# Dilated attention heads laid out query by query, whole row-tiled pairs, and a table of shifts in the instruction order of a one-core transformer kernel

## The chip, the core and the metric

The kernel runs on one core of one Trainium2 chip. The metric is the device time of one execution in microseconds (us), and the time of a kernel is the median of several executions. In the profile the engines are called PE (TensorE, matrix products), PEld (its weight loads), DVE (VectorE), ACT (ScalarE), POOL (GpSimd) and SP (SyncE, which issues the DMA transfers).

## What is computed

A sequence of 512 tokens with 1024 channels goes through two blocks. The first has two layers: mixer AB and then mixer C, each followed by a convolutional FFN and a gated side input (PLE). The second has two hybrid layers. The change rewrites one half of mixer AB, the eight dilated heads of 64 channels; their mathematics is this:

```python
for window, dilation in A_PATTERNS:            # ((128, 1), (512, 4), (2048, 16))
    o, lse = dilated_window_attention(qf, kf, vf, window, dilation)
    outs.append(o)
    lses.append(lse)
w = jax.nn.softmax(jnp.stack(lses), axis=0)
o = jnp.sum(w[..., None] * jnp.stack(outs), axis=0)
```

Three windowed attentions weighted by their log sums are one attention in which a key that lies in n of the three windows counts n times. Both kernels compute it so: before by a factor n on the exponential, after by ln n added to the score. The other half of mixer AB are eight dense latent heads; mixer C is differential attention with 16 score maps.

## The kernel before

The data are feature-major: 128 channels by 512 tokens fill one tile. A large product is made of three products of high and low parts (`h`, `l` are the parts of a weight, staged by DMA into `st`, split by ACT into `h` and by DVE into `l`). The attention of dilated heads is key-major: `attn(j)` handles pair j of heads, j from 0 to 3. It stacks high and low parts of q and k (`stack`), gets each query's row maximum from a first pass of score products (`rowmax`, written to `mt`), transposes the maxima into a row of q (`rows`), and makes the scores a second time, transposed, 128 keys by 512 queries (`attend`). The exponential is then multiplied by the multiplicity `multa` on DVE (`post`), the products with V go to the bank `o`, and the sums of the exponentials come from an addition tree and one product with ones; `finish` divides. Mixer C is query-major: 128 queries by 512 keys, the score products of its two maps run in two 64-row tiles of PE side by side, then exponentials, transpositions through the identity (`identr`) and products with V.

Nothing is issued where it is written. `Rec.add` records every operation with its predecessors, `Rec.price` gives it a cost, and `Rec.order` is a list scheduler: of the operations that are ready on an engine it takes the one with the lowest key, which is the place in the program, or on PE in a small tile mode the lowest of the same mode. `Rec.issue` emits the result, so every row of the trace has line 619 and one goes by the names of the tiles: `d` are the three PSUM banks of dense products, `S` the two of scores, `o` the one of outputs, `m` the two of transpositions and the rest; `s` are slots in SBUF, `sm` small columns. `nc.pair()` links matmuls of two tiles that are to run side by side. The program's orders of steps (`ORDER_AB`, `ORDER_C`, `ORDER_H`) stand at the head of the file.

The stages in the trace of before are: mixer AB 0 to 326 us, FFN and PLE to 757, mixer C to 1036, FFN and PLE to 1470, the hybrid layers to 1961 and to the end.

## Time and profile before

| what | us |
|---|---|
| median of 3 executions | 2468.52 (2467.8 to 2470.66) |
| the profiled execution | 2466.22 |
| its span in the trace | 2464.1 |
| PE busy in the span | 2424.9 (98%) |
| DVE busy | 1462.3 (59%) |
| ACT busy | 1013.8 (41%) |
| POOL busy | 498.1 (20%) |
| mean granted clock of PE | 0.996 |

The profiled execution takes 2.1 us more than its span, and 2.3 us less than the median. A busy PE is one that has an instruction in it: matmuls overlap, a row of the timeline gives a start and a duration that runs into the next instruction, and the distance from one start to the next is what an instruction costs.

### The profile page before, as it was taken

What the parts mean: (1) busy time and instruction counts of PE and PEld (TensorE: products, weight loads), DVE (VectorE), ACT (ScalarE), POOL (GpSimd) and SP (SyncE); (2) the same over time, 40 slices, a digit from 0 to 9 for tenths busy, and PEclk for the clock granted to TensorE, in tenths of its full rate; (3) what the DMA queues carried; (4) which work ended last, traced back from release to release, by engine and by line L of the source; (5) the groups of instructions that cost most, each with busy time, mean ns of one, the idle gap of its engine ahead of it and who ended that gap; (6) DMA issues with size and microseconds to landing.
All of it is one profiled execution on the core that took longest, in us unless ns stands there. A gap on an engine that the chain in (4) does not pass through costs nothing.

```text
span 2464.1 us, 31052 instructions
## 1 busy us (share of the span) xinstructions
PE 2424.9 (98%) x12020; PEld 1934.7 (79%) x12020; DVE 1462.3 (59%) x2461; ACT 1013.8 (41%) x1692; POOL 498.1 (20%) x473
## 2 busy tenths in 40 slices
PE   8999999999999999999999999999999999999998
PEld 6655688888887777888888888776778887767787
DVE  5798675354474756664453676576553556665535
ACT  5554364243353545553342454433333344333332
POOL 1333221010131322211010230311122103111221
PEclk9999999999999999999999999999999999999999
DMA  5102123323323112232232243221232432213331
GB/s 176 52 26 72 59 86 99 98 95 98 100 76 124 52 56 74 85 101 96 94 101 96 86 145 100 78 74 47 93 113 95 167 97 75 77 43 94 113 95 66
DMA packets 73224, 220.26 MB, mean 89 GB/s; under 512 B 9525, under 2 KB 13621, under 8 KB 73078
## 3 DMA queue, kind: packets, MB, share of 16 engines
q1 hardware_dynamic: 73078, 218.30, 27.1%
q8 instruction: 94, 1.54, 0.2%
q14 instruction: 52, 0.43, 0.1%
HBM read 209.87 MB, written 8.39 MB: 89 GB/s over the span
## 4 chain that ended last, share of the span: by engine, by line
PE 89%; DVE 5%; ACT 3%; DMA 1%; issue 1%; POOL 1%; POOLq 0%; DVEq 0%; SPq 0%; ACTq 0%
PE d L619 72%; PE S L619 10%; PE o L619 4%; DVE s L619 4%; PE m L619 3%; ACT s L619 3%; DVE S L619 1%; POOL s L619 1%; DMA st<-in_abin 1%; DVE l L619 0%; DVE mt L619 0%; DVE sm L619 0%; DMA s<-in_p 0%; ACT h L619 0%; ACT sm L619 0%
## 5 line engine op out<-in xcount | busy, mean ns | idle before, releaser
L619 PE MATMUL d<-s,h 128*128 128x512 f32 (+2 forms) x5536 | 1674.6, 381 | 13.4 <-ACT h L619 6.1
L619 PEld LDWEIGHTS d<-s,h 128*128 128x128 f32 (+1 forms) x5536 | 1016.9, 188 | 235.1 <-issue 22.3
L619 PE MATMUL d<-s,l 128*128 128x512 f32 (+1 forms) x2768 | 1047.5, 378 | 0.9 <-DVE l L619 0.7
L619 DVE TENSOR_TENSOR l<-st,h 128x1024 fp32r<-128x1024 f32 (+4 forms) x379 | 473.6, 1252 | 548.0 <-ACT h L619 547.7
L619 ACT ACTIVATE h<-st 128x1024 fp32r<-128x1024 f32 (+4 forms) x379 | 389.2, 1027 | 865.8 <-PE d L619 693.4
L619 POOL TENSOR_TENSOR s<-s,s 128x512 f32<-128x512 f32 (+2 forms) x327 | 406.9, 1249 | 1086.2 <-DVE s L619 671.8
L619 PEld LDWEIGHTS d<-s,l 128*128 128x128 f32 x2768 | 521.4, 188 | 103.4 <-issue 8.0
L619 ACT ACTIVATE s<-s 128x512 f32<-128x512 f32 (+5 forms) x547 | 291.4, 548 | 382.9 <-DVE s L619 273.2
L619 DVE TENSOR_TENSOR s<-s,s 128x512 fp32r<-128x512 f32 (+6 forms) x373 | 215.2, 593 | 95.2 <-ACT s L619 76.4
L619 PE MATMUL S<-s,s 64*128 64x512 f32 (+8 forms) x752 | 197.6, 383 | 3.9 <-DVE mt L619 2.1
L619 PEld LDWEIGHTS S<-s,s 128*128 128x128 f32 (+4 forms) x752 | 112.0, 186 | 78.7 <-ACT s L619 33.7
L619 DVE TENSOR_TENSOR s<-d,s 128x512 f32<-128x512 f32 (+3 forms) x135 | 80.0, 593 | 115.4 <-PE d L619 113.0
L619 POOL TENSOR_SCALAR s<-s 128x512 f32<-128x512 f32 x44 | 29.2, 663 | 579.1 <-ACT s L619 579.1
L619 DVE SCALAR_TENSOR_TENSOR s<-s,s 128x512 f32<-128x512 f32 (+4 forms) x171 | 116.7, 697 | 40.8 <-ACT s L619 40.0
L619 PE MATMUL S<-s,h 128*128 128x256 f32 x704 | 136.3, 285 | 0.0
L619 DVE SCALAR_TENSOR_TENSOR s<-s,d 128x512 f32<-128x512 f32 x152 | 103.9, 683 | 25.6 <-PE d L619 23.2
L619 PEld LDWEIGHTS S<-s,h 128*128 128x128 f32 x704 | 112.4, 193 | 1.6 <-issue 1.6
L619 PE MATMUL o<-s,s 128*128 128x128 f32 (+4 forms) x576 | 101.3, 420 | 5.9 <-DVE s L619 5.1
L619 PE MATMUL S<-s,l 128*128 128x256 f32 x352 | 100.3, 285 | 0.0
L619 ACT ACTIVATE s<-d 128x512 f32<-128x512 f32 (+3 forms) x159 | 89.5, 563 | 23.4 <-PE d L619 23.3
L619 ACT ACTIVATE s<-S 128x512 f32<-128x512 f32 (+5 forms) x154 | 75.1, 510 | 49.8 <-PE S L619 47.9
L619 PEld LDWEIGHTS o<-s,s 128*64 128x64 f32 (+1 forms) x576 | 48.6, 162 | 42.0 <-DVE s L619 17.1
(144 smaller groups left out, 1414.8 us busy)
## 6 DMA issues: line engine op xcount, KB each, us to landing
st<-in_win SPq DMA_DIRECT2D x112, 512.0 KB, 3.4
st<-in_gu SPq DMA_DIRECT2D x88, 512.0 KB, 3.4
st<-in_dn SPq DMA_DIRECT2D x44, 512.0 KB, 3.4
st<-in_pg SPq DMA_DIRECT2D x16, 512.0 KB, 3.4
st<-in_cqk SPq DMA_DIRECT2D x16, 512.0 KB, 3.3
st<-in_wbr SPq DMA_DIRECT2D x16, 512.0 KB, 3.5
st<-in_wo SPq DMA_DIRECT2D x16, 512.0 KB, 3.5
st<-in_abin SPq DMA_DIRECT2D x14, 512.0 KB, 3.8
```

The lines of the kernel that those rows point to most:

```text
L619: getattr(getattr(s.nc, o.eng), o.call)(*[val(v) for v in o.args], **{k: val(v) for k, v in o.kw.items()})
```

## The change

Four things change.

1. `attn(j)` becomes query-major, as mixer C is. For each of four query tiles three pairs of 64-row matmuls write the scores of the two heads into the two `S` banks; DVE adds the mask `maska` and takes the maximum in one instruction, negates it, ACT makes the exponential with its sum. Reciprocal and scaling follow, then transpositions (32 for each pair of heads) and the products with V. The first pass for maxima, the multiplication by `multa`, the addition tree and the products with ones are gone for these heads. The mask is held as four float32 tiles instead of two bfloat16 tables.
2. In `Rec.add` what a later member of a pair waits for is put on its first member as well, so that a pair is not begun before all of it can run.
3. A wait of PE for another engine is taken to be 105 ns longer by the scheduler (`LOAD`), and some prices in `price` are altered.
4. `MOVES`, a table of some 330 entries, shifts the keys of stretches of the program in the list scheduling.

```diff
...
 import math
+import re
 from collections import deque
 from contextlib import ExitStack, contextmanager
 
...
     c["ident"] = np.eye(128, dtype=np.float32)
     f = np.arange(896)[None, :]
     m = _mult(f - p - 384)
-    c["multa"] = m.astype(ml_dtypes.bfloat16)
-    c["maska"] = np.where(m > 0, 0.0, NEG).astype(ml_dtypes.bfloat16)
+    c["maska"] = np.where(m > 0, np.log(np.maximum(m, 1.0)), NEG).astype(np.float32)
     f = np.arange(512)[None, :]
     c["maskc"] = np.where((f - 384 > p), NEG, 0.0).astype(ml_dtypes.bfloat16)
     f = np.arange(128)[None, :]
...
 
 
 SEM = 45.0
+LOAD = 105.0
 PE_LAT = 170.0
 DMA_LAT = 2000.0
 DMA_RATE = 380.0
 DMA_START = 11700.0
+
+
+
+MOVES = """
+820:255v-105 1084:103*+49 722:36v-308 1616:34*+52 1965:4*+14 1574:51*+93 1106:7*+62 84:34*+626 1159:22*-127
...
+15195:155*-447 15233:295t+258 15305:64*+53 15177:311t-527 13187:90*-224 13831:14*-118"""
 
 
 class View:
...
         s.ops.append(o)
         if s.chain is not None and eng == "tensor":
             if s.chain:
+                f = s.chain[0]
+                for p, lag in o.preds.items():
+                    if p < f.i:
+                        f.preds.setdefault(p, lag)
+                for b in o.bufs:
+                    if o in b.firsts and f not in b.firsts:
+                        b.firsts.append(f)
                 o.preds[s.chain[-1].i] = 0.0
             s.chain.append(o)
         return o
...
                 b.firsts.append(o)
 
     def dep(s, o, p, e):
-        o.preds[p] = 0.0 if e == o.eng else SEM
+        o.preds[p] = 0.0 if e == o.eng else s.lag(o)
+
+    @staticmethod
+    def lag(o):
+
+        return SEM + LOAD if o.eng == "tensor" else SEM
 
     def price(s, o, outs, ins):
         e, c, k = o.eng, o.call, o.kw
...
             o.cost = 50 + 0.84 * n if psum else 74 + 0.88 * n
             o.lat = 100
             if "accum_out" in k:
-                o.cost += 185
+                o.cost += 185 if n > 128 else 95
+            o.cost += (0, 100, 310)[isinstance(k.get("scale"), View) + isinstance(k.get("bias"), View)]
             if not outs:
                 o.cost = 1300
         elif e == "vector":
...
                 o.cost = 60 + 0.77 * n
             else:
                 o.cost = 65 + 1.055 * n
+                if n > 64 and any(int(np.prod(v.shape[1:])) == 1 for v in ins):
+                    o.cost += 170
+            o.cost = max(o.cost, 160)
 
             o.lock = bool(ins) and not psum and c != "reciprocal"
         elif e == "gpsimd":
...
         for o in ops:
             o.succs = []
             o.left, o.ready, o.key = len(o.preds), 0.0, o.i
+        for m in MOVES.split():
+            at, n, e, by = re.fullmatch(r"(\d+):(\d+)(.)(.*)", m).groups()
+            for o in ops[int(at):int(at) + int(n)]:
+                if e == "*" or o.eng == {"t": "tensor", "v": "vector", "s": "scalar", "g": "gpsimd", "d": "sync"}[e]:
+                    o.key += int(by)
         for o in ops:
             for p, lag in o.preds.items():
                 ops[p].succs.append((o, lag))
...
                     k.next += 1
                     c.place = b.place
                     for f in c.firsts:
-                        step(f, max(u[1] if u[0] == f.eng != "sync" else u[2] + SEM
+                        step(f, max(u[1] if u[0] == f.eng != "sync" else u[2] + s.lag(f)
                                     for u in (when[x.i] for x in b.users)))
         s.end = max(free.values())
         return out
...
         X = s.xs
         CA, SA, CB, SB = s.rope_tables()
         s.rope_a = (CA, SA)
-        multa, maska = s.slot(BF16), s.slot(BF16)
-        nc.sync.dma_start(multa[:, :896], a["k_multa"])
-        nc.sync.dma_start(maska[:, :896], a["k_maska"])
-        k2s, q2s = s.set_rows(4, 64, 1.0), [s.slot(F32R) for _ in range(4)]
+
+        maska = [s.slot() for _ in range(4)]
+        for q in range(4):
+            nc.sync.dma_start(maska[q], a["k_maska"][:, 384 - 128 * q:896 - 128 * q])
         RQ, RK, lat, OA, OB = {}, {}, [], {}, {}
         V = {"a": [], "b": []}
         L = {}
 
         def prep(j):
-            RQ[j] = s.rope(s.dense("abin", 6 + 2 * j, X), CA, SA, ROT8)
-            yield
-            RK[j] = s.rope(s.dense("abin", 7 + 2 * j, X), CA, SA, ROT8)
-            yield
+
+            for R, t, w in ((RQ, 6 + 2 * j, 0.125), (RK, 7 + 2 * j, 1.0)):
+                r = s.rope(s.dense("abin", t, X), CA, SA, ROT8)
+                hi, lo = s.slot(F32R), s.slot(F32R)
+                nc.scalar.activation(hi, r, AF.Copy, scale=w)
+                nc.vector.scalar_tensor_tensor(lo, r, w, hi, op0=ALU.mult, op1=ALU.subtract)
+                s.free(r)
+                R[j] = (hi, lo)
+                yield
 
         def latent():
             for j in range(5):
...
         done = set()
 
         def attn(j):
-            assert j < 2 or ("a", j - 2) in done
-            rq, rk = RQ.pop(j), RK.pop(j)
-            K, Q, m = [], [], []
-            for e in range(2):
-                k2, q2 = k2s[2 * (j % 2) + e], q2s[2 * (j % 2) + e]
-                K.append((s.stack(rk, 64 * e, False, k2), k2))
-                Q.append((s.stack(rq, 64 * e, True, q2), q2))
-                m.append(s.mt(2, 0.0))
-            s.free(rq, rk)
-            s.rowmax([(Q[e][0], K[e][0], lambda q: maska[:, 384 - 128 * q:896 - 128 * q],
-                       lambda q, e=e: m[e][:, q, 0:1], 512) for e in range(2)])
-            for e in range(2):
-                s.rows(m[e], Q[e][1][64:65], 1)
-            yield
-
-            def post(k, p):
-                nc.vector.scalar_tensor_tensor(p, p, BIG, multa[:, 384 - 128 * k:896 - 128 * k], op0=ALU.min,
-                                               op1=ALU.mult)
-
-            r = s.attend([([(K[e][0], Q[e][0]), (K[e][1][:65], Q[e][1][:65])], None, post) for e in range(2)],
-                         [lambda k, h=2 * j + e: V["a"][k][:, 64 * h:64 * h + 64] for e in range(2)], 0.125, False)
-            for e in range(2):
-                s.free(K[e][0], Q[e][0])
-            done.add(("a", j))
+
+            (qh, ql), (kh, kl) = RQ.pop(j), RK.pop(j)
+            P = [[], []]
+            l = s.sm.tile([128, 4, 2], F32, tag="asum", name=f"asum{j}", bufs=2)
+            for i in range(2):
+                for q in (2 * i, 2 * i + 1):
+                    c = slice(128 * q, 128 * q + 128)
+                    ps = [s.bank("S") for _ in range(2)]
+                    with s.nc.pair():
+                        for t, (x, y) in enumerate(((qh, kh), (ql, kh), (qh, kl))):
+                            for e in range(2):
+                                R = slice(64 * e, 64 * e + 64)
+                                nc.tensor.matmul(ps[e], lhsT=x[R, c], rhs=y[R], start=t == 0, stop=t == 2)
+                    m = s.small(2, tag="am")
+                    for e in range(2):
+                        nc.vector.tensor_tensor_reduce(ps[e], ps[e], maska[q], scale=1.0, scalar=-BIG, op0=ALU.add,
+                                                       op1=ALU.max, accum_out=m[:, e:e + 1])
+                    nc.vector.tensor_scalar(m, m, -1.0, None, op0=ALU.mult)
+                    for e in range(2):
+                        p = s.slot()
+                        nc.scalar.activation(p, ps[e], AF.Exp, bias=m[:, e:e + 1], accum_out=l[:, q, e:e + 1])
+                        P[e].append(p)
+                if i == 1:
+                    s.free(qh, ql, kh, kl)
+                nc.vector.reciprocal(l[:, 2 * i:2 * i + 2], l[:, 2 * i:2 * i + 2])
+                for q in (2 * i, 2 * i + 1):
+                    for e in range(2):
+                        nc.scalar.activation(P[e][q], P[e][q], AF.Copy, scale=l[:, q, e:e + 1])
+                yield
+            po = s.bank("o")
+            for k in range(4):
+                T = []
+                for e in range(2):
+                    pt = s.bank("m")
+                    for q in range(4):
+                        nc.tensor.transpose(pt[:, 128 * q:128 * q + 128], P[e][q][:, 128 * k:128 * k + 128], s.ident)
+                    t = s.slot()
+                    if e:
+                        nc.vector.tensor_copy(t, pt)
+                    else:
+                        nc.scalar.activation(t, pt, AF.Copy)
+                    T.append(t)
+                s.pair(po, lambda e, h=2 * j: V["a"][k][:, 64 * (h + e):64 * (h + e) + 64], T, 0, k == 0, k == 3)
+                s.free(*T)
+            s.free(*P[0], *P[1])
             if j == 3:
-                s.free(*V["a"], *k2s, *q2s, multa, maska)
-            yield
-            OA[j] = s.finish(*r)
+                s.free(*V["a"], *maska)
+            OA[j] = s.split(po)
             yield
 
         KB = []

```

Three places of the order of instructions, before and after. The first is PE in mixer C. `S` are the score banks of a query tile, `d` a dense product that is made meanwhile; the six rows of `S` of one tile belong to three pairs. Before:

```order
L619 MATMUL S_6499<-s_6367,s_6315 128x512
L619 MATMUL d_6461<-s_6186,h_6360 128x512
L619 MATMUL S_6502<-s_6367,s_6315 128x512
L619 MATMUL S_6499<-s_6367,s_6326 128x512
L619 MATMUL S_6502<-s_6367,s_6326 128x512
L619 MATMUL S_6499<-s_6376,s_6315 128x512
L619 MATMUL S_6502<-s_6376,s_6315 128x512
L619 MATMUL d_6461<-s_6193,h_6360 128x512
```

After, for the tile that stands at this place:

```order
L680 MATMUL d_6527<-s_6151,h_6428 128x512
L680 MATMUL S_6537<-s_6435,s_6383 128x512
L680 MATMUL S_6539<-s_6435,s_6383 128x512
L680 MATMUL S_6537<-s_6435,s_6394 128x512
L680 MATMUL S_6539<-s_6435,s_6394 128x512
L680 MATMUL S_6537<-s_6444,s_6383 128x512
L680 MATMUL S_6539<-s_6444,s_6383 128x512
L680 MATMUL d_6527<-s_6129,l_6437 128x512
```

Before, a row of `d` stands inside the first pair; after, the six rows stand together. Over the whole of mixer C the 32 tiles stand in 51 runs of 64-row matmuls before, with 36 rows (18 pairs) that have another instruction between them and their partner; after, in 32 runs with none.

The second is PE in the first hybrid layer: `o` is the bank in which two heads' products with V are added up, in column tiles of PE. Before:

```order
L619 MATMUL d_14042<-s_12287,l_13944 128x512
L619 MATMUL d_14042<-s_12313,h_13930 128x512
L619 MATMUL d_14042<-s_12327,h_13930 128x512
L619 MATMUL o_14091<-s_14108,s_12588 64x256
L619 MATMUL o_14091<-s_14105,s_12588 64x256
L619 MATMUL d_14042<-s_12313,l_13944 128x512
L619 MATMUL o_14091<-s_14129,s_12594 64x128
L619 MATMUL o_14091<-s_14125,s_12594 64x128
L619 MATMUL d_14042<-s_12320,h_13930 128x512
```

After:

```order
L680 MATMUL S_14352<-s_13724,s_14255 128x256
L680 MATMUL d_14216<-s_12459,l_14158 128x512
L680 MATMUL d_14188<-s_12335,l_14066 128x512
L680 MATMUL o_14360<-s_14270,s_12557 64x512
L680 MATMUL o_14360<-s_14261,s_12557 64x512
L680 MATMUL o_14360<-s_14285,s_12568 64x384
L680 MATMUL o_14360<-s_14276,s_12568 64x384
L680 MATMUL o_14360<-s_14301,s_12703 64x256
L680 MATMUL o_14360<-s_14289,s_12703 64x256
L680 MATMUL o_14360<-s_14313,s_12710 64x128
L680 MATMUL o_14360<-s_14299,s_12710 64x128
```

Before, the four pairs of `o` are separated by rows of `d` and `S`; after, they follow one another. Over both hybrid layers there are 50 runs of column-tiled matmuls before and 32 after, in mixer AB 30 and 21 (four of these nine are the products with ones that no longer exist). In mixer AB runs of transposed row maxima fall from 61 to 22, 32 such matmuls being gone.

The third is DVE in mixer AB, in the stretch in which PE has little but attention left. `s_188` is `multa`, `o_1529` the output bank of a pair of dilated heads, `mt` the maxima of a dense pair. Before:

```order
L619 SCALAR_TENSOR_TENSOR s_1594<-s_1594,s_188 128x512
L619 SCALAR_TENSOR_TENSOR s_1603<-s_1603,s_188 128x512
L619 TENSOR_TENSOR s_1625<-s_1424,s_1493 96x512
L619 TENSOR_TENSOR s_1629<-s_1454,s_1527 96x512
L619 SCALAR_TENSOR_TENSOR s_1633<-o_1529,s_1613 128x512
L619 TENSOR_TENSOR s_1613<-m_1600,s_1613 128x512
L619 SCALAR_TENSOR_TENSOR s_1633<-s_1613,s_1633 128x512
L619 TENSOR_REDUCE mt_930<-S_1611 128x1
```

After, with `m` a bank of transposed exponentials that is copied out, `d` a dense product of the rope, `asum` the sums of the exponentials, and `o_1627` the output bank of a pair:

```order
L680 TENSOR_REDUCE mt_79<-S_1668 128x1
L680 RECIPROCAL asum_1384<-asum_1384 128x4
L680 TENSOR_REDUCE mt_81<-S_1677 128x1
L680 TENSOR_REDUCE mt_79<-S_1684 128x1
L680 COPY s_1694<-m_1681 128x512
L680 STREAM_SHUFFLE s_1700<-d_1552 96x512
L680 TENSOR_REDUCE mt_79<-S_1698 128x1
L680 TENSOR_REDUCE mt_81<-S_1706 128x1
L680 TENSOR_TENSOR s_1718<-d_1552,s_482 96x512
L680 TENSOR_REDUCE mt_81<-S_1716 128x1
L680 TENSOR_REDUCE mt_79<-S_1725 128x1
L680 TENSOR_TENSOR s_1740<-o_1627,s_1720 128x512
```

Before, the reading of the output bank stands behind eight multiplications by `multa` (the last two of them are the first rows here) and two additions; after, there is no multiplication, and the reading stands between maxima of the dense heads.

## Rows read from the trace of the kernel before

**Rows 1.** The page: span, busy time by engine, the chain that ended last.
```profile
span 2464.1 us, 31052 instructions
...
PE 2424.9 (98%) x12020; PEld 1934.7 (79%) x12020; DVE 1462.3 (59%) x2461; ACT 1013.8 (41%) x1692; POOL 498.1 (20%) x473
...
PE 89%; DVE 5%; ACT 3%; DMA 1%; issue 1%; POOL 1%; POOLq 0%; DVEq 0%; SPq 0%; ACTq 0%
```

**Rows 2.** Windows: stretch, length, busy of PE, PEld, DVE, ACT, POOL, clock, DMA.
```profile
124.00:186.00 62.00, 55.93 (x248) 34.98 (x248) 56.57 (x107) 32.50 (x58) 21.80 (x22) 0.98 0.10 32
...
757.00:1036.00 279.00, 278.60 (x1523) 221.78 (x1522) 172.37 (x310) 134.23 (x312) 72.49 (x54) 1.00 0.23 74
...
1961.00:2464.10 503.10, 491.48 (x2373) 388.15 (x2371) 286.34 (x535) 175.34 (x280) 89.60 (x75) 0.99 0.27 86
186.00:190.00 4.00, 4.00 (x12) 1.16 (x10) 3.25 (x5) 0.63 (x1) 2.54 (x2) 0.52 0.69 222
299.20:302.40 3.20, 3.20 (x17) 3.20 (x16) 1.23 (x4) 0.00 (x0) 2.19 (x3) 0.50 0.02 5
```

**Rows 3.** PE's waits from 0 to 350 us: total, times, longest.
```profile
PE d L619 <- ACT s L619: 2.8, 1, 2.8
PE S L619 <- DVE mt L619: 2.1, 2, 1.7
```

**Rows 4.** PE's timeline in mixer C, an unbroken group: start, duration, operation.
```profile
827.55 1.03 PE L619 MATMUL m<-identr,s 128*128 128x128 f32 x8
828.52 0.96 PE L619 MATMUL S<-s,s 64*128 64x512 f32 x6
829.41 2.05 PE L619 MATMUL o<-s,s 128*128 128x128 f32 x16
```

**Rows 5.** PE's timeline in mixer C, a group that is broken up.
```profile
831.39 0.50 PE L619 MATMUL S<-s,s 64*128 64x512 f32 x1
831.82 0.44 PE L619 MATMUL m<-identr,s 128*128 128x128 f32 x2
832.19 0.96 PE L619 MATMUL S<-s,s 64*128 64x512 f32 x5
833.08 0.44 PE L619 MATMUL m<-identr,s 128*128 128x128 f32 x2
```

**Rows 6.** PE's timeline in mixer AB, column-tiled runs of four.
```profile
169.57 1.08 PE L619 MATMUL o<-s,s 128*64 128x512 f32 x4
170.58 0.97 PE L619 MATMUL S<-s,s 128*128 128x512 f32 x3
```

**Rows 7.** PE's timeline in mixer AB, a column-tiled run of eight.
```profile
120.79 1.94 PE L619 MATMUL o<-s,s 128*64 128x512 f32 x8
122.66 0.50 PE L619 MATMUL d<-s,h 128*128 128x512 f32 x1
```

**Rows 8.** PE's timeline in mixer AB around one transposition of row maxima.
```profile
97.85 0.63 PE L619 MATMUL d<-s,h 128*128 128x512 f32 x2
98.32 0.39 PE L619 MATMUL S<-s,s 128*128 128x512 f32 x1
...
98.89 0.40 PE L619 MATMUL d<-s,h 128*128 128x512 f32 x1
```

**Rows 9.** PE's timeline in mixer AB at its longest wait.
```profile
185.41 5.85 PE L619 MATMUL o<-s,s 128*64 128x512 f32 x16 [4.54 <-DVE s L619]
```

**Rows 10.** DVE's timeline just before that wait ends.
```profile
178.54 4.90 DVE L619 SCALAR_TENSOR_TENSOR s<-s,s 128x512 f32<-128x512 f32 x8
...
184.67 0.69 DVE L619 SCALAR_TENSOR_TENSOR s<-o,s 128x512 f32<-128x512 f32 x1
```

**Rows 11.** DVE's groups by form from 60 to 326 us: busy, mean ns, idle before.
```profile
L619 DVE SCALAR_TENSOR_TENSOR s<-s,s 128x512 f32<-128x512 f32 x40 | 32.0, 845 | 1.4 <-ACT s L619 1.1
...
L619 DVE CUSTOM_DVE_ANT_0 S<-S,s 128x512 f32<-128x512 f32 x30 | 20.4, 705 | 0.4
```

**Rows 12.** ACT's groups by form over the whole span.
```profile
L619 ACT ACTIVATE s<-S,sm 128x512 f32<-128x512 f32 x64 | 43.5, 684 | 30.6 <-DVE sm L619 30.5
```

More of the change, by code (lines that the diff above doesn't have):

```diff
@@ new lines @@
+1077:2t-261 560:47*-252 1165:24t+37 617:6t-333 1668:27t-195 2123:5*+10 2081:210v-9 1181:34*-242 1467:2*-37
+1122:21*-213 1138:255t+17 1106:70*+151 4567:114*-71 6914:44*-527 6986:17t-94 6524:388v+762 4439:113*-732 6522:9*-420
+6571:41*-122 6856:145s+27 4659:120*+18 11506:211*-159 11557:268t+112 9341:21*+59 9329:17*-358 11048:2*+164
+12116:121*-137 10142:11*+282 11476:219*-403 12013:123*-422 10129:38*+309 10967:329*-183 9364:9s+80 10520:71*+320
+11099:138*-7 11723:30*+164 10705:204s+404 10702:10*-85 10426:287*+132 11016:104*+104 13293:5*+470 11068:315*-5
@@ new lines @@
+9885:37v-689 11487:360*+9 13253:47*+305 12107:75*-12 13057:29*-216 11163:100s+73 10324:91*-175 10537:63t-2
+11386:59*+414 10474:150*+2 9315:140*-41 13264:36*+13 13291:9t+1 11296:10*+4 11554:154*+58 11253:244*+479
+13083:74*-18 13106:29*+12 13097:6*+66 9340:22*-11 11653:128*-14 11431:11*-68 10612:14*-92 11546:106*+18
+11968:365*-15 11736:14*+21 11808:27*-252 12036:317*+277 11523:8s+349 10627:6t+5 11594:2*+241 11550:291*+8
+12038:156*-24 12115:10*+95 11566:326*+13 11466:10t-309 11787:188t+12 9362:3*+677 11300:251*+60 11581:216s+251
@@ new lines @@
+10527:2*-659 10657:116s+82 12842:63*-330 11780:5*-384 9335:27*-14 11462:108s+660 11744:40*-14 10402:372s-198
+10743:32*-67 10502:128s-611 11838:86*+151 11616:23*-177 11843:37*-681 11462:299t+83 10634:71*+6 10796:64*-70
+9259:335t-25 9269:246v-347 11466:299t-83 11540:383t-19 11795:12*-378 10776:51t+121 11906:16*+158 9279:90*-1
+11521:4t-678 9274:6*+5 9272:29*-7 11654:87*+21 9359:12*+25 11592:25*+263 11550:3*-83 11641:18*-355 12098:7*-158
+11527:63t-50 11523:156*+26 11829:43*+67 10502:329*+9 10814:14*-6 9400:18*+9 10643:2*+72 13102:3v+486 12136:51*-466
@@ new lines @@
+12095:6*-193 11461:48*+26 10633:76*-8 14344:47*+171 14326:192*+42 13594:190t+107 14029:99*+186 13597:196*+5
+13855:3*+133 14965:21*+120 14584:11*-78 13835:56t+105 14225:25*+217 13506:184t-407 14628:2*+19 13681:233*+249
+13164:198s+273 13388:67*-161 13171:206*-123 13366:31t+459 13699:62*-85 13293:119t+114 13350:74t-775 14150:353*+5
+15075:68*-372 13303:21*+181 13288:164v-351 13273:78*-302 16256:3*+175 15098:200*+27 13289:21*+314 13521:5t+25
+16216:4*+178 15274:21*+27 13355:3*+775 13315:335t-165 14395:53*+23 13782:323t-7 15169:389t+24 14707:41*-577
```

13 lines of the change are left out of this document (added).

## Prediction, made before the changed kernel was run

> **What bounds the kernel now.** The page comes first: PE is busy for 2424.9 of 2464.1 us, and the chain that ended last runs over PE for 89% [rows 1]. So the time is the length of PE's queue of work plus its few waits, and a change counts by what it does to PE's instructions, their density, and the waits between them. DVE, at 59% over the span, is no bound, but that is a mean. The windows show where it isn't one: from 124 to 186 us, in mixer AB, DVE is busy for 56.57 of 62 us, and there PE has 6 us idle [rows 2]. In mixer C PE is idle for 0.4 of 279 us, so there only density can give anything; in the last hybrid layer it is idle for 11.6 of 503.1 us [rows 2]. Next the timeline, read from one start to the next, since durations overlap: in C an unbroken group of score pairs, and one that another instruction breaks [rows 4, 5]; in AB column-tiled runs of four and eight rows [rows 6, 7]. Last the waits of AB: one of 4.54 us for DVE [rows 9], one of 2.8 us for ACT, two of 2.1 us together for maxima on DVE [rows 3].
>
> **Prices on PE.** Two plain rows and the start behind them are 0.47 us apart (97.85 to 98.32), 0.23 us a row [rows 8]. Eight transpositions take from 827.55 to 828.52; with 0.10 us for the switch to 64-row tiles that is 0.109 us each [rows 4]. Six score rows of an unbroken group run as three streams of two rows side by side, and take 0.89 us: 3 x 0.23 and 0.20 of switching inside the run [rows 4]. With some 0.10 us at each end (16 V rows of 0.109 are 1.74 us, but fill 1.98 from 829.41 to 831.39 between two such runs [rows 4, 5]) a run costs its streams x 0.23 plus 0.40. An unbroken group is then 1.09 us. The broken one has a lone row first (831.39 to 831.82, 0.43 us), then five rows (0.89 us) [rows 5]: four streams in two runs, 1.72 us. A broken pair costs 0.63 us more.
>
> A column-tiled run of four rows (one pair of products) is 1.01 us from start to start [rows 6], and 1.21 with 0.10 us at either end, taken from the row behind it, where three plain rows need 0.90 us instead of 0.69 [rows 6]. Eight rows are 1.87 us [rows 7], 2.07 with ends. Joining two runs saves 2 x 1.21 - 2.07 = 0.35 us. One transposed column of maxima between plain rows adds 0.57 - 2 x 0.23 = 0.11 us [rows 8].
>
> **The dilated heads' work on PE.** Removed: 96 score rows of 128 or 65 rows of PE (64 of the first kind, 32 of the second; the first pass for maxima is among them), 96 x 0.23 = 22.1 us; 32 transposed columns, 3.5; four products with ones, 4 x 1.21 = 4.8. Together 30.4 us. Added: 16 groups of three row-tiled pairs, 16 x 1.09 = 17.4; 128 transpositions, 14.0. Together 31.4. The V products are the same. So the rewriting is no gain on PE: **+1.0 us**.
>
> [...]
>
> **The order.** In mixer C 18 broken pairs become whole and 19 runs disappear: 18 streams x 0.23 and 19 x 0.40 are **-11.7 us**. In the hybrid layers 18 column-tiled runs are joined to others, 18 x 0.35 = **-6.3 us**; in AB five more, **-1.7 us**. These are counts of the order of instructions with prices of the trace, and PE's idle time there is small, so what makes PE's queue shorter makes the stage shorter, unless the new order waits.
>
> **The waits of mixer AB.** At 180.9 us PE waits 4.54 us for the one `o` bank [rows 9]. DVE frees it with `s<-o`, which starts at 184.67, behind eight multiplications by the multiplicities (4.90 us from 178.54) [rows 10]. Behind PE's waiting instruction stand all its other matmuls. The 16 rows that follow take 5.85 us instead of 2 x 1.94 [rows 7, 9], 2.0 us more, at a granted clock of 0.52, about the lower level [rows 2]; and 1.7 us of the maxima's waits [rows 3] follow. The place costs 8.2 us. After, the multiplications don't exist. DVE loses 32 of them at 0.845 us [rows 11], 27 us, and 48 additions and the like of 64 or 128 rows by 512 (0.69, as the row at 184.67 [rows 10]), 33 us; it gains 28 copies, subtractions and splittings at 0.69, 19 us, and 24 instructions on two or four columns. These have no row here; between nothing and 0.69 I take 0.2 us, since they hold so little data: 5 us. The 32 additions of the mask take the place of 32 others of the same form at 0.705 [rows 11]. DVE gets some 36 us lighter, where it was over nine tenths busy. I take **-6** of the 8.2 us: the bank is then read behind maxima of the dense heads, so some wait is left. A second place waits 2.8 us for ACT [rows 3] and then runs for 3.2 us at a clock of 0.50 [rows 2], 1.6 us lost, 4.4 in all; nothing in the change aims at it, only the stages ahead of it shift, so between 0 and 4.4 I take **-2**. Rows that start late by less than the page calls idle, in a stage with so busy a DVE, I put at **-3** (between 0 and the 6 us of idle time from 124 to 186).
>
> **What costs nothing.** ACT gets 32 scalings and 32 exponentials with bias (0.684 us [rows 12]) in place of as many plain ones and the logarithms: at 41% [rows 1] and 32.5 of 62 us in that stretch [rows 2] PE's own work covers that; uncovered, the scalings would be 32 x 0.684 = 22 us. The masks are 0.59 MB more on SP's queue, ahead of later weights. At the 222 GB/s that the queue has moved [rows 2] that is 2.7 us, hidden behind the first dense products; if not, +2.7.
>
> **Sum.** 1.0 - 11.7 - 6.3 - 1.7 - 6 - 2 - 3 = -29.7. Against the profiled execution's 2466.2 that is 2436.5; the median shown is 2.3 us above that execution, so I forecast **2438.8 us**. A measurement of this kernel can tell about 0.2%, 4.9 us.
>
> **Rivals.**
> *The gains go further* (0.22). The waits that I left are taken too: the 2.2 us of the first place, the 2.4 of the second, and four fifths of the 11.6 us of idle time in the last hybrid layer [rows 2], 9.3 us. 2438.8 - 14 = 2424.8. For it: the scheduler now counts a wait of PE as longer and puts other work into it. Against it: what costs little in such a count needn't on the chip.
>
> *The order gives its gains back* (0.17). A dense order leaves less independent work to fill a wait: half of the 18.0 us of C and the hybrid layers comes back as waits of PE, and in AB the 11 us of waits only move, since the dilated heads now follow one another with nothing but attention on PE. 2438.8 + 9 + 11 = 2458.8.
>
> *The query-major chain becomes the bound: slower* (0.04). A query tile holds both `S` banks from its first matmul to the second exponential: 0.89 us on PE [rows 4], 2 x 0.705 on DVE [rows 11], 2 x 0.684 on ACT [rows 12], 3.7 us, and five short reads and a negation at 0.2, by estimate 4.8. The order puts eight transpositions (0.9 us), one or two V pairs (1.2 each) and some dense rows between two groups, 3.5 to 3.8 us. Were PE to wait for the difference of about 1 us at each of the 16 tiles, that takes 16 us off the gain; at 1.9 us a tile the gain is gone, and above 2.2 the kernel is slower by over 0.2%: at 2.5 us it is 2438.8 + 40 = 2479. Against it: the dense heads' groups and the next pair's V products can go between, and DVE is lighter. [...]
>
> *Transpositions at their full length* (0.02). If each cost what it lasts, 1.03 - 7 x 0.109 = 0.27 us [rows 4], and not the step of 0.109, 128 x 0.16 = 20 us are added: 2459.
>
> *The change does nothing* (0.03): the shifted keys act only where several operations are ready, and what they close up reopens elsewhere; 2466 to 2470.
>
> **How the numbers follow.** The forecast, 2430 to 2448 by its own bounds, has 0.52. The range reaches down past the first rival's middle, to 2413, where nearly all waits of before would be gone, and up to the second rival's middle, 2458: 0.52 + nine tenths of 0.22 + half of 0.17 are 0.80. Faster by over 0.2%, below 2463.6, are the forecast, the first rival, nearly all of the second and the fourth, 0.92; no change 0.04, slower 0.04.
>
> **What would show it.** In the profile after: AB's waits for DVE without one above 2 us, and no stretch at half the clock behind it; C's busy PE about 12 us shorter with 64-row matmuls in runs of six; the hybrid layers shorter by some 3 us each. It would be wrong if PE's waits in AB name ACT or DVE at the dilated heads' score groups, each by a microsecond or more, or if mixer C shows idle time of PE.

## The result: 2402.9 us, twice the gain that was forecast

| | before | after |
|---|---|---|
| median, us (the runs of one chip) | 2469.59 (4 runs, 2467.8 to 2470.7) | 2402.89 (4 runs, 2402.59 to 2404.78) |
| span of the profiled execution, us | 2464.1 | 2401.0 |

The ratio is 0.9732, with a 95% interval of 0.9715 to 0.9749. The kernel is 66.7 us faster; 29.7 were forecast, and the time lies below the range, which ended at 2413. The spans of the two profiled executions, which are cut into stages below, differ by 63.1 us.

The page of the changed kernel has these rows in place of [rows 1]:

```profile
span 2401.0 us, 31174 instructions
PE 2378.2 (99%) x12100; PEld 1927.6 (80%) x12100; DVE 1433.7 (60%) x2433; ACT 1017.1 (42%) x1732; POOL 489.7 (20%) x453
...
PE 95%; DVE 2%; ACT 2%; issue 1%; DMA 1%; SPq 0%; POOL 0%; POOLq 0%; DVEq 0%; ACTq 0%
```

PE has 80 matmuls more and is busy for 46.7 us less. Its idle time only falls from 39.2 to 22.8 us. So most of the gain lies inside what the page calls busy. There the prediction had put 18.7 of its 29.7 us, by the runs of small tile modes and the heads' own work alone. Cut into stages (a stage begins with the first matmul on its first weights), the two traces give, in us:

| stage | before | after | difference | forecast |
|---|---|---|---|---|
| mixer AB | 326.2 | 304.6 | -21.6 | -11.7 |
| FFN and PLE, first layer | 378.1, 53.1 | 373.0, 49.9 | -8.3 | 0 |
| mixer C | 278.7 | 267.4 | -11.3 | -11.7 |
| FFN and PLE, second layer | 378.0, 55.6 | 373.0, 49.2 | -11.4 | 0 |
| hybrid layers | 491.4, 503.0 | 485.4, 498.5 | -10.5 | -6.3 |

The windows of the stages show what kind of time went. First the kernel before, mixer AB and the first FFN (columns as in [rows 2]):

```profile
0.00:326.20 326.20, 307.26 (x1393) 208.43 (x1394) 248.70 (x412) 158.69 (x256) 98.19 (x107) 0.98 0.25 79
326.20:704.30 378.10, 377.62 (x1837) 318.35 (x1836) 198.22 (x266) 150.28 (x208) 58.43 (x62) 1.00 0.29 94
```

Then the changed kernel, mixer AB, the first FFN and mixer C:

```profile
0.00:304.60 304.60, 296.26 (x1468) 209.39 (x1469) 215.20 (x385) 166.53 (x295) 83.13 (x87) 1.00 0.27 87
304.60:677.60 373.00, 373.00 (x1838) 317.22 (x1837) 195.76 (x264) 149.45 (x209) 58.74 (x61) 1.00 0.29 94
...
727.50:994.90 267.40, 267.05 (x1522) 216.57 (x1520) 176.87 (x316) 135.56 (x317) 73.03 (x56) 1.00 0.24 77
```

In mixer AB PE's idle time falls from 18.9 to 8.3 us, and the granted clock rises from 0.98 to 1.00. DVE got 33.5 us lighter there, near the forecast of 36. In the FFN the same matmuls (1837 and 1838) keep PE busy for 4.6 us less: there the page had shown no idle time to take away, 0.5 of 378 us.

**Where the FFN's 5 us lay.** The timeline of PE in the kernel before, just behind the layer norm that opens the FFN:

```profile
327.60 0.84 PE L619 MATMUL d<-s,h 128*128 128x256 f32 x2
328.28 0.28 PE L619 MATMUL d<-s,l 128*128 128x256 f32 x1
328.60 0.85 PE L619 MATMUL d<-s,h 128*128 128x256 f32 x2
329.28 0.28 PE L619 MATMUL d<-s,l 128*128 128x256 f32 x1
329.54 0.39 PE L619 MATMUL d<-s,h 128*128 128x256 f32 x1
```

Three matmuls take 1.00 us from one start to the next (327.60 to 328.60); in the changed kernel, shown further down, such rows start 0.11 us apart (305.38 to 305.49). The weight loads of the same stretch show why:

```profile
328.06 0.19 PEld L619 LDWEIGHTS d<-s,h 128*128 128x128 f32 x1 [0.27 <-DVE s L619]
328.16 0.19 PEld L619 LDWEIGHTS d<-s,l 128*128 128x128 f32 x1
328.60 0.19 PEld L619 LDWEIGHTS d<-s,h 128*128 128x128 f32 x1 [0.24 <-ACT s L619]
329.06 0.19 PEld L619 LDWEIGHTS d<-s,h 128*128 128x128 f32 x1 [0.27 <-DVE s L619]
```

Each load in these rows that needs a new part of the layer norm's output waits 0.24 to 0.27 us for ACT or DVE, and the matmul's duration runs over the gap (the rows of `d<-s,h` from 326.8 to 349 us last 337 ns in the mean, those of `S<-s,h` 284), so PE counts as busy. Over the whole first FFN these waits of the loads add up to 3.8 us before (total, times, longest):

```profile
PEld d L619 <- ACT s L619: 2.1, 11, 0.2
PEld d L619 <- DVE s L619: 1.4, 6, 0.3
PEld o L619 <- POOL s L619: 0.3, 1, 0.3
```

In the changed kernel's first FFN the same view has no row at all. Here is the same place in that kernel:

```profile
304.56 0.28 PE L680 MATMUL S<-s,h 128*128 128x256 f32 x1
304.68 0.52 PE L680 MATMUL d<-s,h 128*128 128x256 f32 x2
305.03 0.40 PE L680 MATMUL d<-s,l 128*128 128x512 f32 x1
305.27 0.28 PE L680 MATMUL S<-s,h 128*128 128x256 f32 x1
305.38 0.27 PE L680 MATMUL S<-s,l 128*128 128x256 f32 x1
305.49 0.28 PE L680 MATMUL S<-s,h 128*128 128x256 f32 x1
```

The rows of 512 columns are a product of the side input, which needs nothing of the layer norm; it has been kept back for this place, and a second output tile (`S`) is made in turn with the first (`d`) from the start (before, the first row of `S` comes at 329.76). Two windows of 22.2 us from here on, of the kernel before and of the changed one, say the same in one line each:

```profile
326.80:349.00 22.20, 21.72 (x142) 18.01 (x141) 15.25 (x37) 16.39 (x38) 3.06 (x4) 1.00 0.08 25
```

```profile
304.50:326.70 22.20, 22.20 (x179) 21.90 (x179) 14.88 (x38) 17.73 (x40) 3.10 (x4) 1.00 0.08 25
```

PE is busy to within half a microsecond in both, but 142 matmuls against 179 were started, and the weight loads were busy for 18.01 against 21.90 us. The reader should take the count, not PE's busy time, as the measure here.

### The profile page after: what moved, and what is told of

Same layout as the page of the kernel before. It is cut to its first block, busy times and chain, and to the rows that moved or that the text cites. A ratio compares the mean times of both kernels' runs of the same rounds, so it can differ in the third digit from the quotient of the medians.

```text
span 2401.0 us, 31174 instructions
## 1 busy us (share of the span) xinstructions
PE 2378.2 (99%) x12100; PEld 1927.6 (80%) x12100; DVE 1433.7 (60%) x2433; ACT 1017.1 (42%) x1732; POOL 489.7 (20%) x453
## 4 chain that ended last, share of the span: by engine, by line
PE 95%; DVE 2%; ACT 2%; issue 1%; DMA 1%; SPq 0%; POOL 0%; POOLq 0%; DVEq 0%; ACTq 0%
PE d L680 76%; PE S L680 11%; PE m L680 4%; PE o L680 4%; ACT s L680 1%; DVE s L680 1%; DVE sm L680 0%; DVE l L680 0%; DMA s<-in_x 0%; DVE S L680 0%; DMA s<-in_pos 0%; ACT h L680 0%; SPq L680 0%; DVE mt L680 0%; POOL s L680 0%
## 5 line engine op out<-in xcount | busy, mean ns | idle before, releaser
L680 PE MATMUL d<-s,h 128*128 128x512 f32 (+1 forms) x5536 | 1659.8, 380 | 2.8 <-ACT s L680 1.8
L680 PEld LDWEIGHTS d<-s,h 128*128 128x128 f32 x5536 | 1013.7, 188 | 205.9 <-issue 17.5
L680 DVE TENSOR_TENSOR l<-st,h 128x1024 fp32r<-128x1024 f32 (+3 forms) x379 | 467.0, 1236 | 511.5 <-ACT h L680 504.9
L680 POOL TENSOR_TENSOR s<-s,s 128x512 f32<-128x512 f32 (+3 forms) x319 | 407.0, 1281 | 1118.4 <-DVE s L680 550.1
L680 ACT ACTIVATE s<-s 128x512 f32<-128x512 f32 (+6 forms) x515 | 270.4, 542 | 356.7 <-DVE s L680 264.9
L680 DVE TENSOR_TENSOR s<-s,s 128x256 fp32r<-128x256 f32 (+6 forms) x337 | 198.7, 603 | 82.9 <-ACT s L680 68.8
L680 PE MATMUL S<-s,s 64*128 64x512 f32 (+10 forms) x752 | 173.0, 378 | 2.7 <-ACT s L680 2.1
L680 PEld LDWEIGHTS S<-s,s 64*128 64x128 f32 (+5 forms) x752 | 103.0, 185 | 63.4 <-ACT s L680 20.8
L680 DVE TENSOR_TENSOR s<-d,s 128x512 f32<-128x512 f32 (+4 forms) x135 | 79.6, 592 | 101.3 <-PE d L680 99.0
L680 PE MATMUL d<-h,s 128*128 128x512 f32 (+1 forms) x252 | 79.4, 377 | 5.7 <-ACT s L680 5.7
```

Of the source, the lines that this page charges most:

```text
L680: getattr(getattr(s.nc, o.eng), o.call)(*[val(v) for v in o.args], **{k: val(v) for k, v in o.kw.items()})
```

## The experiments

The stage lengths are cut as in the table above and read in each run's trace, which is one execution, so they carry the clock of that execution; times are medians, and all ratios are to the kernel before on the same chip, in square brackets with their interval. Four parts can be set one by one: the heads, the correction of pairs, the lag (with the prices), and the table (292 entries, not some 330 as was said ahead). The first theory was that the longer lag had closed the small waits of the FFNs, since it concerns every wait of PE; its rival, that the table had.

### One part alone on the kernel before

The lag alone:

```diff
...
-        o.preds[p] = 0.0 if e == o.eng else SEM
+        o.preds[p] = 0.0 if e == o.eng else s.lag(o)
...
```

> The kernel before with one change to its scheduler: a wait of PE for another engine counts 150 ns instead of 45. Theory lag: the two FFN and two PLE stages, which got 19.7 us shorter in the changed kernel (378.1, 53.1, 378.0 and 55.6 us to 373.0, 49.9, 373.0 and 49.2) without a single entry of the table of shifts for the FFNs, got it from this count; then this kernel shows FFN stages of 373 us and PLE stages near 50, and some 20 us less in all, 2445 to 2452. Rival table: those stages gained from what stands before them or from prices; then they stay at 378 and 53 to 56, and the time at 2465 to 2470.

(The table does have entries there: seven stand at the opening of the first FFN, numbers 2073 to 2125, and six about the opening of the second, 6522 to 6986.)

Measured: 2464.96, 0.9988 [0.9978, 0.9997]. The FFN stages are 377.8 and 377.7 us, the PLE stages 53.1 and 55.7, and in the first FFN the loads still wait 3.6 us. The theory fell: the lag by itself doesn't make the FFNs shorter.

The correction of pairs alone:

```diff
             if s.chain:
+                f = s.chain[0]
+                for p, lag in o.preds.items():
+                    if p < f.i:
+                        f.preds.setdefault(p, lag)
+                ...
                 o.preds[s.chain[-1].i] = 0.0
```

> The kernel before with the correction of pairs alone: the first matmul of a pair waits for what any of them waits for. Theory: the 18 broken pairs of mixer C are its doing, so mixer C falls from 278.7 to about 267 us (18 x 0.23 + 19 x 0.40 = 11.7 by the prediction's prices) and nothing else moves by more than 2 us: 2457 in all. Rival: the table closed the pairs up; then mixer C keeps most of its 278.7 us, and the time is within 5 us of 2469.

Measured: 2456.34, 0.9953 [0.9938, 0.9968], 11.5 us. Mixer C takes 269.2 us, 9.5 less; no other stage moves by more than 1 us, and the 51 runs of 64-row matmuls in its order are 32. So this gain is the correction's, at about the prices of [rows 4, 5].

The heads alone:

```diff
...
-        multa, maska = s.slot(BF16), s.slot(BF16)
+        maska = [s.slot() for _ in range(4)]
...
         def attn(j):
...
-            rq, rk = RQ.pop(j), RK.pop(j)
+            (qh, ql), (kh, kl) = RQ.pop(j), RK.pop(j)
...
```

> The query-major dilated heads in the scheduler of before, without correction, lag, prices and table. By the prediction's terms: the heads' own work on PE is worth +1.0 us, the waits of mixer AB -11, so 2459, all in mixer AB. Theory heads: the whole 21.6 us by which mixer AB got shorter (326.2 to 304.6) belong to the heads: 2448. Rival order: without the new order a score group holds both banks while PE has nothing else to do, and mixer AB is no shorter than 326 us or longer: 2468 or above.

Measured: 2471.54, 1.0012 [1.0001, 1.0024]. Mixer AB takes 329.1 us, 2.9 more than before, although DVE is 43 us lighter in it. This is its window, and its waits of PE behind the first 40 us:

```profile
0.00:329.10 329.10, 313.87 (x1473) 216.65 (x1473) 205.21 (x384) 168.60 (x296) 81.83 (x87) 0.97 0.25 80
```

```profile
PE d L618 <- ACT s L618: 2.7, 1, 2.7
PE m L618 <- ACT s L618: 1.4, 2, 0.7
PE S L618 <- ACT s L618: 1.1, 1, 1.1
PE o L618 <- DVE s L618: 0.6, 1, 0.6
...
```

The wait of 4.5 us for the bank `o` is gone, as forecast, and PE's idle time falls by 3.7 us: behind the first 40 us its waits fall from 11.5 to 7.3 us, though those for ACT rise from 3.9 to 5.2. But PE's busy time is 6.6 us longer. Of these, 3.4 are the lower clock (8.5 us lost to it in mixer AB against 5.1, counted as in the last section), and the prediction had +1.0 for the heads' own work. So the relief of DVE gave nothing in all.

### The changed kernel with one part taken away

The table emptied:

```diff
-MOVES = """
...
-15195:155*-447 15233:295t+258 15305:64*+53 15177:311t-527 13187:90*-224 13831:14*-118"""
+MOVES = ""
```

> The changed kernel with an empty table of shifts; heads, correction of pairs, lag and prices stay. Theory lag: FFN and PLE stages keep their 373 and 50 us, mixer C keeps its 267 to 270, and only mixer AB and the hybrid layers, where most entries stand, lose: 2412 to 2425. Rival table: most of the 66.7 us are the table's, 2440 or above.

Measured: 2449.31, 0.9919 [0.9902, 0.9935]. The table is worth 46.4 us, the rest of the change 18.5 on this chip. Mixer AB takes 331.2 us, the FFNs 376.6 and 377.9, the PLE stages 53.8 and 54.2, mixer C 266.9, the hybrid layers 489.2 and 502.7. In the time the rival held. The trace doesn't say, though, that the FFNs are as before: in the first one the 18 small waits of the weight loads are one of 1.9 us, without an entry of the table. What this is worth, and why it hardly shows in these lengths, is told under the table by place.

The lag taken away, with the whole table:

```diff
-LOAD = 105.0
+LOAD = 0.0
```

> The changed kernel with the whole table, but the lag of PE's waits as before (45 ns). Theory lag needed: the table was made for that lag, and without it the small delays behind the layer norms and in mixer AB come back: 2420 or above. Rival: the table alone holds the order, and the lag is worth what it was by itself, 3 us: 2403 to 2408.

Measured: 2446.31, 0.991 [0.9895, 0.9925]: 43.4 us are lost, in mixer AB (325.3), the first FFN (378.2) and the hybrid layers (490.7 and 504.7) above all; part of it is a lower clock in this execution (0.993 in the mean, against 0.999 in the changed kernel's profiled one). A lag that is worth 3 us by itself is worth 43 under the table. Without the lag the whole table is only 3.0 us below the empty table with the lag.

The prices of ACT and DVE taken away, with table and lag:

```diff
-                o.cost += 185 if n > 128 else 95
+                o.cost += 185
...
-            o.cost = max(o.cost, 160)
```

> The changed kernel with the whole table and the lag, but with the old prices of ACT and DVE operations. Theory: a table of shifts holds only for the model under which it was found, so any change of the model gives most of it back: 2425 or above, mostly in mixer AB and the hybrid layers, where prices of exponentials with sums and of small DVE operations count. Rival: only the lag of PE matters: 2403 to 2410.

Measured: 2444.05, 0.99 [0.9885, 0.9915]. 41.2 us are lost, but not in the same places: only 4.6 in mixer AB (309.2), as much in each FFN (377.9 and 377.6), 4 to 6 in each PLE stage, 3.9 in mixer C (271.3), most in the last hybrid layer (510.1, 11.6 more). The table holds for the model under which it was found: a small change of the model gives nearly all of it back.

### The table by place

Only the 95 entries of mixer AB, and only the 197 behind it:

```diff
-MOVES = """
-820:255v-105 1084:103*+49 722:36v-308 1616:34*+52 1965:4*+14 1574:51*+93 1106:7*+62 84:34*+626 1159:22*-127
...
+MOVES = """
+820:255v-105 1084:103*+49 722:36v-308 1616:34*+52 1965:4*+14 1574:51*+93 1106:7*+62 84:34*+626
...
```

(the entries whose number is below 2032; in the other kernel, those from 2032 on)

> The changed kernel with the 95 entries of the table that lie in mixer AB, the other 197 left out. Theory table by place: each entry works where it stands, so mixer AB gets its 304.6 us (331.2 with the empty table) and the later stages keep the lengths that they have with the empty table: 2449.3 - 26.6 = 2423. Rival heads as a state: mixer AB's gain depends on what is pulled from behind it, too; then it ends at 310 us or later.

> The changed kernel with the 197 entries behind mixer AB. Theory table by place: the FFNs at 373 and 373 us, the PLE stages at 50 and 49, the hybrid layers some 8 us shorter than with the empty table, mixer AB at 331: 2449.3 - 20 = 2429. Rival: these stages were shorter because mixer AB left another state behind; then they stay at 377 to 378 and 54, and the time is above 2440.

Measured: 2427.36, 0.9838 [0.9821, 0.9854], mixer AB 306.6 us; and 2426.61, 0.9829 [0.9814, 0.9844], mixer AB 328.0, FFNs 373.0 and 373.0, PLE stages 49.9 and 49.2, hybrid layers 485.4 and 498.8. The two halves are 22.0 and 22.7 us and add up to 44.7 of the 46.4. In the main the gain stands where the entries stand. One thing was not expected: with the entries of mixer AB alone the FFN and PLE stages also got shorter, by 1.4 to 3.0 us each.

That is not the order. In the first PLE, the second FFN and the second PLE PE's instructions stand in the same order in both kernels, one by one. The granted clock differs. Here is the second FFN, and 12 us behind its opening, first with the empty table and then with the entries of mixer AB:

```profile
1028.50:1406.40 377.90, 376.16 (x1838) 320.16 (x1837) 196.62 (x267) 148.44 (x208) 60.90 (x62) 0.99 0.27 94
1036.00:1048.00 12.00, 11.41 (x70) 11.41 (x71) 6.37 (x15) 5.18 (x11) 1.69 (x3) 0.72 0.14 44
```

```profile
998.60:1373.60 375.00, 373.26 (x1837) 317.26 (x1836) 196.56 (x266) 148.45 (x207) 61.01 (x62) 1.00 0.30 94
1006.00:1018.00 12.00, 11.27 (x94) 11.24 (x95) 7.63 (x18) 7.98 (x17) 1.84 (x3) 1.00 0.14 44
```

So at the full clock the rules (the correction of pairs, the lag and the prices, under the new heads) bring these three stages from 53.1, 378.0 and 55.6 us to 50.8, 375.0 and 52.8 without an entry there, and the entries bring them to 49.9, 373.0 and 49.2: of 14.6 us, 8.1 are the rules' and 6.5 the table's. In the execution with the empty table the lower clock took 7.3 of the 8.1 back.

The 197 entries in the kernel before, with nothing else:

```diff
+MOVES = """
+2075:8*-41 2026:4*-686 2033:3s+246 2063:27t+652 2023:70*+536 2073:5*+10 2031:210v-9 4517:114*-71
...
+        for m in MOVES.split():
...
+                    o.key += int(by)
```

> The kernel before, its heads, scheduler rules and prices as they were, with the same 197 entries behind mixer AB (all numbers of the program lowered by 50, the length by which its mixer AB is shorter). Theory: interleaving at the two layer norms is what the FFN entries do, and it needs neither the new heads nor the longer lag; FFN stages at 373 to 374 us, PLE stages near 50, the hybrids 5 to 10 us shorter, mixer C unchanged: 2440. Rival: the entries fit only the order that the lag and the prices make; the stages get less than a third of it or get longer: 2462 or above.

Measured: 2473.03, 1.0013 [1.0003, 1.0023], FFNs 378.5 and 378.2. So the entries do nothing for the FFNs under the old rules.

### Do the heads matter?

The old heads under the new rules, without table, and with the 197 entries behind mixer AB:

```diff
 LOAD = 105.0
...
-            (qh, ql), (kh, kl) = RQ.pop(j), RK.pop(j)
+            rq, rk = RQ.pop(j), RK.pop(j)
```

> The kernel before with the correction of pairs, the lag and the prices, without new heads and without table. With the empty table the changed kernel takes 2449.3 us; the only difference is the heads. Theory heads neutral: the rewriting is worth nothing by itself, 2449 to 2455 here. Rival heads gain once pairs and lag are right: 2460 or above. Rival heads lose: below 2445.

> The kernel of the run before it with the 197 entries behind mixer AB, their numbers lowered by 50. In the scheduler of before the same entries gained nothing (2473). Theory lag and table together: with the lag they bring the FFNs to 373 us and the PLE stages to 50, whatever the heads: 21 to 25 us below the kernel without them. Rival: they depend on the state that the new heads leave behind: less than 10 us.

Measured: 2451.0, 0.9928 [0.9911, 0.9945], beside 2449.3 with new heads; and 2427.48, 0.983 [0.9812, 0.9849], beside 2426.6. In both settings the heads are worth 1 or 2 us, less than can be told. In mixer AB there may be more, hidden by the clock: with its share taken off, as in the last section, the empty table gives 314.2 us with the new heads and 318.3 with the old, an estimate from one execution each. The entries work here (-23.5 us), so what they need is the rules, not the heads.

The old heads with shifts of their own in mixer AB:

This is the kernel of the run before it with another table: the 197 entries, and shifts that were found for these heads, written out as 2991 entries, nearly every operation of mixer AB with a shift of its own.

```diff
-MOVES = """
...
+MOVES = """
...
```

> The key-major heads of the kernel before, with the correction of pairs, lag and prices, the 197 entries behind mixer AB, and shifts of their own for mixer AB, found for these heads by half an hour of trying random shifts and keeping those with which the scheduler's own end falls. Without shifts in mixer AB this kernel takes 2427.5 us, with mixer AB at 330 us. Theory order: the 22 to 27 us that the table brings in mixer AB are a matter of the order, not of the heads; mixer AB falls to 305 to 312 us and the time to 2402 to 2410. Rival heads: only query-major heads can be laid so that PE doesn't wait; mixer AB stays above 320 us, the time above 2417.

Measured: 2410.41, 0.9767 [0.9748, 0.9785], mixer AB 308.3 us instead of 329.9. The time is 0.4 us above what I had given; mixer AB speaks for the order. Its window:

```profile
0.00:308.30 308.30, 297.85 (x1388) 207.12 (x1388) 240.61 (x411) 158.71 (x255) 98.61 (x107) 1.00 0.26 82
```

DVE carries 240.61 us here, 25 more than in the changed kernel, and PE's idle time is 10.5 us against 8.3. The heavy DVE doesn't stand in the way of most of the gain once the order is right. The changed kernel stays 7.5 us ahead, 3.7 of them in mixer AB; whether by its heads or by its own search was not separated.

### The price of a transposition, and one more search

Each of the 128 new transpositions made twice, in the kernel with the empty table:

```diff
-                        nc.tensor.transpose(pt[:, 128 * q:128 * q + 128], P[e][q][:, 128 * k:128 * k + 128], s.ident)
+                        for _ in range(2):
+                            nc.tensor.transpose(pt[:, 128 * q:128 * q + 128], P[e][q][:, 128 * k:128 * k + 128], s.ident)
```

> The changed kernel with an empty table and with each of the 128 new transpositions made twice, so that their number doubles and nothing else is asked of any engine. Theory step price: 0.109 us each, 14 us more than with the empty table, 2463, or less where they fall into waits of mixer AB. Rival full length: 0.275 us each, 35 us more, 2484.

Measured: 2453.05, 0.9938 [0.9922, 0.9954], 3.7 us above the kernel with the empty table; mixer AB is 331.9 us instead of 331.2. A run of sixteen in this kernel, and one of eight in the changed kernel:

```profile
187.68 1.97 PE L645 MATMUL m<-identr,s 128*128 128x128 f32 x16
```

```profile
171.72 1.09 PE L680 MATMUL m<-identr,s 128*128 128x128 f32 x8
```

Eight more take 0.88 us more, 0.11 each. The duration of one is longer: the 296 rows of `m<-identr,s` in the changed kernel's trace last 274 ns in the mean. That is about the length which the rival priced; it is not what one in a row costs. Why even the 14 us of the step price hardly show in the time is told in the last section.

The table developed further over the whole program, which is again only another table:

```diff
-MOVES = """
...
+MOVES = """
...
```

> The changed kernel with its table developed further in the same way for half an hour, over the whole program. Theory: what is left of PE's waits after the table is little, and the scheduler's model no longer tells what the chip will do, so the time stays within 5 us of 2402.9. Rival: more search brings more, 2397 or less.

Measured: 2405.67, 0.9743 [0.9729, 0.9758], 2.8 us above the changed kernel, though the scheduler's own end had fallen; the two intervals overlap. The table has 15076 entries now, most of them for one operation. Mixer AB is 304.8 us, the second FFN 369.4, its PLE 53.3. What one stage gains another loses; no version here beats the changed kernel.

## Why the prediction was too small

**Mixer C: right.** 11.7 us forecast, 11.3 in the trace of the changed kernel, and the correction of pairs alone shows 9.5 in the stage and 11.5 in the median.

**The heads' own work on PE (+1.0): right in kind.** The heads alone make the kernel 3.7 us slower, part of it by a lower clock (3.4 us in mixer AB); under the new rules they are worth nothing that can be told in the time. The step price of 0.109 us holds for the 128 doubled transpositions (last section).

**"The waits of mixer AB" failed.** The prediction gave -6 for the bank `o` and -3 for a lighter DVE to the new heads, and -2 for a wait for which nothing in the change seemed to aim. The wait did go, DVE did get lighter, and the heads alone gained nothing: a part of the waits moved to ACT (5.2 us for it instead of 3.9), and the stage ran at a lower clock (0.97 against 0.98). In the changed kernel idle time and clock gave 15.7 us of mixer AB's 21.6 (10.6 of idle time, and 5.1 for the clock: the missing share of full clock in each stretch of 10 us, added up), and most of that came with the table, with the new heads or the old. The other 5.9 us are busy time at the full clock, where the sum had only the five joined runs (-1.7) and the heads (+1.0); they were not taken apart. So the step had the wrong cause for the waits, and a size that was too small.

**The FFN and PLE stages had no term at all; this is the larger miss, 19.7 us.** This is the step that failed most. The prediction said of mixer C, where PE shows no idle time, that "only density can give anything", and then priced density by tile modes alone; the FFNs, which are as busy, got no term, and no reason was given. It read idle time from PE's rows, and the small waits there are on the weight loads' rows. In the four stages the loads wait 18.0 us for other engines before (3.8 and 3.7 in the FFNs, 5.5 and 5.0 in the PLE stages) and 2.9 after. The rows of the first PLE, before:

```profile
PEld d L619 <- ACT s L619: 3.6, 12, 1.7
PEld d L619 <- DVE s L619: 1.5, 5, 0.5
PEld o L619 <- POOL s L619: 0.4, 1, 0.4
```

and after:

```profile
PEld d L680 <- ACT s L680: 1.6, 1, 1.6
PEld S L680 <- DVE l L680: 0.3, 1, 0.3
```

The 15.1 us by which these waits fell would account for most of the 19.7; on PE's own rows only 3.6 us of idle time went in these four stages. The rules and the table share the gain, as shown under the table by place.

**Hybrid layers: the order's runs were rightly counted, the size too small.** 6.3 forecast, 10.5 measured; the table is worth 8.0 of it (991.9 us in the two layers with it empty, 983.9 with it; with it empty none of the 18 runs is joined), the rules the rest. Idle time of PE in the first of them fell by 1.9 us; the remainder was not taken apart.

**The rivals.** The one that carried the gains further had the right direction; at 2424.8 it too stopped at idle time that the page shows. The one by which the order gives its gains back did not happen here. With the lag or the prices taken away 41 to 43 us are lost, but because the table no longer fits its model; that dense order leaves too little work to fill waits was not shown. The slower rival, the score groups that hold both banks, didn't come (its chain adds up to 4.9 us, not 4.8, which changes nothing): PE's waits for ACT at score banks in mixer AB of the changed kernel are 0.6 us in two waits. On the weight loads' rows the 64-row score groups wait 5.1 us for ACT there, in ten waits of which none is a microsecond long. So what the holding of both `S` banks costs is small here at most; no run separates it from other waits.

**What stays open.** Which of the rules removes the small waits in the FFNs was not found: the lag alone and the correction of pairs alone don't, and the prices alone were not tried. Which of the seven entries at the opening of the first FFN does the rest was not tried either. Why the lower clock falls on some stretches and not on others isn't known.

## What to carry to other kernels

A busy engine is not a dense one (here 142 matmuls against 179 in 22.2 us, with PE busy for 21.72 and 22.20 of them): before a stage that is 99% busy is put down as having nothing to give, count its matmuls in a stretch where the inputs come late, and read the waits of the weight loads. Before a stage of one execution is compared with that of another, compare their clocks (the second FFN took 377.9 us at 0.99 and 375.0 at 1.00 in the same order). A table of shifts found by search was worth much here, but only for the cost model that it was found with: change a lag or a price and it has to be searched again. Relief on an engine that is waited for gave nothing here by itself (DVE 43 us lighter in mixer AB, and the stage 2.9 us longer); it took another order.

## What the runs showed that was not expected

PE's clock fell while PE was busy all the time. In the kernel with the empty table PE's timeline at 112 us shows a group of scores and then sixteen matmuls with one column each:

```profile
112.72 0.96 PE L645 MATMUL S<-s,s 64*128 64x512 f32 x6
113.62 1.95 PE L645 MATMUL m<-meanq,s 128*128 128x1 f32 x16
```

and its windows show the granted clock falling behind it, to 0.85 and then 0.50, with PE busy for 3.00 of each 3.00 us:

```profile
111.00:114.00 3.00, 3.00 (x18) 2.00 (x17) 0.28 (x1) 1.39 (x2) 0.00 (x0) 1.00 0.34 98
114.00:117.00 3.00, 3.00 (x20) 2.70 (x20) 2.51 (x7) 2.23 (x6) 0.38 (x1) 0.85 0.00 0
117.00:120.00 3.00, 3.00 (x13) 2.15 (x13) 0.28 (x1) 0.00 (x0) 0.64 (x1) 0.50 0.16 49
```

Added up over mixer AB in stretches of 10 us, the clock costs 17.0 us in this kernel's profiled execution, 5.1 before, 8.5 with the heads alone, 11.9 with the old heads under the new rules, and nothing in the changed kernel or with the old heads and their own table. With the transpositions doubled it costs 3.4. With these shares taken off, mixer AB takes 314.2 us with the empty table and 328.5 with the transpositions doubled: the 14.3 us between them are the step price of 128 transpositions, and they hardly show because 13.6 us less were lost to the clock.

These are single executions, and that with the empty table is the slowest of its four, 5.0 us above the median. But the kernels differ in all of theirs: the mean granted clock is 0.986 to 0.991 with the empty table and 0.997 to 0.999 in the changed kernel. By these means the clock takes some 28 us of the one and some 4 of the other, so by this estimate about half of the 46.4 us that the table brings is clock. That the changed kernel runs at a higher clock than with the empty table is shown. That the order inside a stage alone sets it is not: the second FFN above ran in the same order at two clocks (0.99 and 1.00). And that the added transpositions kept the clock up, and not the other order that came with them, is argued and not shown.
